# Splitting three weight matrices one layer earlier, and moving a substitution's transfers to the GpSimd queue

## The chip, the cores and the metric

The kernel runs on one core of a Trainium2 chip. The metric is device time in microseconds. The kernel before was timed three times: median 1341.9 us, from 1339.78 to 1342.38 us.

## The reference, cut to what matters

A trunk of four residual sub-layers (token mixer, FFN, token mixer, FFN) on 512 tokens of width 1024, in float32:

```
for i in range(2):
    hn = rms_norm(h, norm_mix_g[i])
    h = h + (sgu_mixer if i == 0 else rwkv7_mixer)(hn, ...)
    h = h + conv_ffn(rms_norm(h, norm_ffn_g[i]), ...)     # (silu(gate) * val) @ w_down, gate, val = conv3(h @ w_up)
return rms_norm(h, norm_final_g)

def rwkv7_mixer(h, ...):             # 16 heads of 64
    xx = token_shift(h) - h
    r, k, v = (h + xx * mu[0]) @ w_r, (h + xx * mu[2]) @ w_k, (h + xx * mu[3]) @ w_v
    w, a, g = low_rank(h + xx * mu[1]), low_rank(h + xx * mu[4]), low_rank(h + xx * mu[5])
    # for each token and head, state S of 64x64:
    #   S = S diag(decay) + (S (-kk)) (kk * a)^T + v k^T ;  y = S r
    y = group_norm(y) * ln_w + ln_b + bonus
    return (y * g) @ w_o
```

The change touches the first FFN (FFN0) and the RWKV-7 mixer behind it.

## The kernel before, in words

**Layout and precision.** Activations stand with 128 features on the partitions and 512 tokens along the row; D = 1024 is 8 such tiles. A float32 product is made of three matmuls on TensorE (`mm3`, lines 240 to 246): both operands are split into a rounded high part and a remainder, and high by high, high by low and low by high are added up. Three matmuls of 128x512 belong to each 128x128 block of a weight.

**Weights.** `weights` (line 221) loads a 512 KB piece from DRAM by the DMA queue of ScalarE (ACT) into `w32` (two buffers), and `split` (line 197) makes the parts of each 512 columns: ACT casts to `wh` (line 205), VectorE (DVE) subtracts to `wl` (line 206), with four buffers each. `Ahead` fetches one weight before it is used.

**FFN0** makes 44 tiles of the up projection, 24 matmuls each, with convolution and gate on DVE and ACT behind them (lines 463 to 470), and then 8 tiles of the down projection.

**RWKV.** `rwkv_first` makes the low-rank terms and r. `rwkv_main` (line 656) is made of generators that `weave` (line 1127) interleaves by `RATES`: a main stream, a side stream and `fill`, which supplies matmuls.

- `projections` is the fill: k and v (16 weights). Each tile of v is followed by `value`: its transposed store (line 738, `vtd`) and a bonus term (line 752). The last four tiles of v belong to head pairs 4 to 7, which the second scan uses.
- `pairs`: for each pair of heads p = 0 to 7 the decay, operands and products of 64-token chunks. They are stored to DRAM scratch by SyncE's queue (SP): `std`, `lpd` (lines 844, 845) and `btd` (lines 856, 858).
- `invert(g)` inverts triangular 64x64 blocks for one group of four pairs: it loads the diagonal 32x32 blocks as `li` (line 898) and the others as `lm` (line 900), substitutes in 31 steps of two DVE operations (lines 910, 911) on a tile `tt`, transposes (lines 918, 919), stores `tt` (line 915), multiplies on TensorE (line 930), copies (line 932) and stores `lm` (line 935). Both groups use the same buffers.
- `scan(g)` runs the recurrence of a group in 8 chunks. Each loads `st`, `vu`, `pt` (from the inverted `lpd`) and `cbt` by SP (lines 954 to 960), and alternates four sets of matmuls (lines 978, 982, 991, 998, 1003) with copies on DVE and ACT. `finish` normalizes two chunks at a time and, twice per group, multiplies by the gate (line 1045 stands in it).
- `project` multiplies by wo, half before all gates are there (group 0), half after (group 1).

The order is: pairs 0 to 3; pairs 4 to 7 with inversion 0 at the side; scan 0 with inversion 1 at the side and the last four tiles of v as fill; scan 1 with `project` as fill; the rest of `project`; FFN1. Tile's scheduler turns that program order into one list of instructions for each engine, and every engine works its list in order.

## Time and profile before

| | |
|---|---|
| three runs, median | 1341.9 us (1339.78 to 1342.38) |
| the profiled execution's own time | 1336.87 us |
| its span in the trace | 1335.0 us |
| TensorE busy | 1269.7 us, 95% of the span |
| DVE, ACT, POOL busy | 842.3, 605.6 and 140.8 us |
| the chain that ended last | 79% TensorE, 8% DVE, 2% ACT, 2% DMA |

TensorE (PE) fills nearly the whole span; the profile page's forty slices show it below 90% in the RWKV stage, from about 600 to 965 us, and at the very ends. A time on the page is a duration in us, or a mean in ns for one instruction. "PE ... x112" counts matmuls; the granted clock (PEclk) is 1.00 at full speed; the DMA share is the mean busy share of the 16 DMA engines and can come out above 1. A name ending in q (SPq, ACTq) is an engine's issuing of a transfer. A bracket behind an instruction tells how long its engine had been idle and what released it.

### The profile page before, as it was taken

The numbers are of one execution on the slowest core, as the hardware profiler recorded it, in microseconds if no ns is written. First come the engines' busy times: TensorE is split into PE (matmuls) and PEld (weight loads), VectorE is DVE, ScalarE is ACT, GpSimd is POOL, SyncE is SP. The second block draws the span as 40 slices with busy tenths as digits, with TensorE's granted clock in tenths as the row PEclk, the third lists the DMA queues.
The fourth block names the chain that finished last, engine by engine and source line by source line (L and its number), as shares of the span: only waits on it lengthen the run. The fifth ranks groups of instructions, "written<-read, shape, count | busy, mean of one in ns | idle before, by whom it ended". The sixth has DMA issues, their size and how long they took to land.

```text
span 1335.0 us, 19041 instructions
## 1 busy us (share of the span) xinstructions
PE 1269.7 (95%) x7490; PEld 1022.9 (77%) x7490; DVE 842.3 (63%) x1349; ACT 605.6 (45%) x1060; POOL 140.8 (11%) x152
## 2 busy tenths in 40 slices
PE   8999999999999999999989848798999999999996
PEld 6778888888888888777766636676888888888886
DVE  5565477777773335957979476556577777772223
ACT  5444354544443333667875424222454545452221
POOL 3100200000000001311210003232300000000001
PEclk9999999999999999999989869899999999999998
DMA  7232333323333333235866796962223333332322
GB/s 260 82 110 79 95 95 95 95 95 97 101 99 103 118 103 99 83 114 128 199 153 171 160 202 151 242 177 79 79 95 95 95 96 99 103 93 87 103 88 75
DMA packets 135786, 156.63 MB, mean 117 GB/s; under 512 B 64976, under 2 KB 100944, under 8 KB 135696
## 3 DMA queue, kind: packets, MB, share of 16 engines
q10 hardware_dynamic: 30688, 101.07, 24.9%
q1 hardware_dynamic: 105008, 54.34, 16.9%
q8 instruction: 59, 0.97, 0.3%
q14 instruction: 31, 0.25, 0.1%
HBM read 130.74 MB, written 24.64 MB: 116 GB/s over the span
## 4 chain that ended last, share of the span: by engine, by line
PE 79%; DVE 8%; ACT 2%; DMA 2%; issue 2%; POOL 1%; SPq 0%; ACTq 0%; DVEq 0%; POOLq 0%
PE mm L244 8%; PE mm L245 8%; PE mm L246 8%; PE e L244 5%; PE e L246 5%; PE e L245 5%; PE us L244 5%; PE us L246 5%; PE us L245 5%; PE aux L244 5%; PE aux L246 5%; PE aux L245 5%; DVE pr L910 1%; DVE tt L911 1%; PE us L978 1%
## 5 line engine op out<-in xcount | busy, mean ns | idle before, releaser
L205 ACT CAST wh<-w 128x512 fp32r<-128x512 f32 (+1 forms) x393 | 239.3, 613 | 441.5 <-PE mm L245 121.0
L206 DVE TENSOR_TENSOR wl<-w,wh 128x512 fp32r<-128x512 f32 (+1 forms) x385 | 267.0, 696 | 206.0 <-ACT wh L205 200.7
L244 PE MATMUL mm<-mxh,wh 128*128 128x512 f32 x424 | 175.1, 413 | 2.7 <-DVE rt L754 2.0
L245 PE MATMUL mm<-mxl,wh 128*128 128x512 f32 x424 | 169.8, 400 | 0.3 <-DVE mxl L1051 0.3
L246 PE MATMUL mm<-mxh,wl 128*128 128x512 f32 x424 | 168.3, 397 | 1.4 <-DVE wl L206 1.4
L271 POOL TENSOR_TENSOR ss<-ss,sq 128x512 f32<-128x512 f32 x30 | 40.4, 1347 | 777.5 <-issue 594.7
L244 PEld LDWEIGHTS mm<-mxh,wh 128*128 128x128 f32 x424 | 80.7, 191 | 25.3 <-issue 4.5
L246 PEld LDWEIGHTS mm<-mxh,wl 128*128 128x128 f32 x424 | 80.5, 190 | 19.2 <-DVE wl L206 2.1
L245 PEld LDWEIGHTS mm<-mxl,wh 128*128 128x128 f32 x424 | 80.7, 190 | 17.7 <-issue 1.4
L465 ACT ACTIVATE cv<-z,par 128x512 f32<-128x512 f32 x88 | 71.7, 817 | 30.4 <-DVE z L463 30.4
L244 PE MATMUL us<-mxh,wh 128*128 128x512 f32 (+1 forms) x216 | 84.5, 391 | 0.1
L244 PE MATMUL e<-mxh,wh 128*128 128x512 f32 x216 | 84.5, 391 | 0.0
L246 PE MATMUL us<-mxh,wl 128*128 128x512 f32 (+1 forms) x216 | 84.1, 389 | 0.0
L245 PE MATMUL us<-mxl,wh 128*128 128x512 f32 (+1 forms) x216 | 84.1, 389 | 0.0
L245 PE MATMUL e<-mxl,wh 128*128 128x512 f32 x216 | 84.0, 389 | 0.0
L246 PE MATMUL e<-mxh,wl 128*128 128x512 f32 x216 | 84.0, 389 | 0.0
L466 DVE SCALAR_TENSOR_TENSOR cv<-z,par,cv 128x512 f32<-128x512 f32 x88 | 66.0, 752 | 24.3 <-ACT cv L465 24.3
L244 PE MATMUL aux<-mxh,wh 128*128 128x512 f32 x208 | 81.2, 391 | 0.1
L246 PE MATMUL aux<-mxh,wl 128*128 128x512 f32 x208 | 81.1, 390 | 0.0
L245 PE MATMUL aux<-mxl,wh 128*128 128x512 f32 x208 | 80.9, 389 | 0.0
L467 DVE SCALAR_TENSOR_TENSOR cv<-z,par,cv 128x512 f32<-128x512 f32 x88 | 66.0, 752 | 2.9
L244 PEld LDWEIGHTS e<-mxh,wh 128*128 128x128 f32 x216 | 40.6, 188 | 8.8 <-issue 0.5
(1062 smaller groups left out, 2499.0 us busy)
## 6 DMA issues: line engine op xcount, KB each, us to landing
w<-in_wup ACTq DMA_DIRECT2D x88, 512.0 KB, 3.6
w<-in_wdn ACTq DMA_DIRECT2D x32, 512.0 KB, 3.6
st<-std SPq DMA_DIRECT2D x16, 512.0 KB, 6.4
w<-in_wdn ACTq DMA_DIRECT2D x16, 384.0 KB, 3.1
w<-in_wsu ACTq DMA_DIRECT2D x8, 512.0 KB, 3.9
w<-in_wso ACTq DMA_DIRECT2D x8, 512.0 KB, 3.6
w<-in_wk ACTq DMA_DIRECT2D x8, 512.0 KB, 4.3
std<-ar SPq DMA_DIRECT2D x16, 256.0 KB, 4.6
```

The source lines that it names most:

```text
L205: nc.scalar.copy(hi[r, :n], src)
L206: (lo_eng or nc.vector).tensor_tensor(lo[r, :n], src, hi[r, :n].bitcast(F32), ALU.subtract)
L244: mm(acc, wh, xh, start=first, stop=False)
L245: mm(acc, wh, xl, start=False, stop=False)
L246: mm(acc, wl, xh, start=False, stop=last)
L271: nc.gpsimd.tensor_tensor(self.ss, self.ss, self.sq, ALU.add)
L465: nc.scalar.activation(c, z[:, 2:], AF.Identity, scale=cw(2, i), bias=self.p("conv_b", l * 44 + i))
L466: nc.vector.scalar_tensor_tensor(c, z[:, 1:T + 1], cw(1, i), c, ALU.mult, ALU.add)
L467: nc.vector.scalar_tensor_tensor(c, z[:, 0:T], cw(0, i), c, ALU.mult, ALU.add)
L910: V.tensor_tensor(q, a, b, ALU.mult)
L911: V.tensor_tensor(tt[:, 0:nj, j + 1:32], tt[:, 0:nj, j + 1:32], q, ALU.add)
L978: nc.tensor.matmul(us[H[hd], 0, i, :], st[:, i, hd, 0:C], vu[:, i, hd, :], start=True, stop=True)
```

## The change

1. **Parts beside FFN0.** `make_parts` is advanced once for each weight of FFN0 (44 times in the up, 4 times in the down projection). A step loads 512 columns of wk, wv or wo by SP, splits them on ACT and DVE and stores both parts to a DRAM scratch `wd`. Its three tiles have one buffer each. In RWKV `parts` loads them: two DMAs on ACT's queue for each 512 columns, into `wh`/`wl`, and every third time into a `w32` buffer. Casts and subtractions of these 24 weights leave the RWKV stage (for wo, half of the subtractions were on POOL), and twice the bytes are loaded there.
2. **Substitution transfers on POOL.** `li` and `lm` are loaded for each pair of heads as it gets ready, by POOL's queue, three DMAs for each pair; the stores of `tt` and `lm` go there too. `lpd` is laid out pair by pair. The two inversions form one side stream.
3. **One store of `bt`** with rows of 512 bytes instead of three stores with rows of 256.
4. **Order.** The loads of scan 0's first chunk, 9 steps of fill and 18 of inversion stand before scan 0; the gates' weights are loaded at the end of the fill; the last `finish` of a scan is carried on in what follows; the reloading of h is written at the head of `project`; the rates change.

```
-RATES = ((1.9, 2), (1.9, 6, 2.2), (0.8, 2, 2), (0.6, 2))
+RATES = ((1.9, 2), (1.9, 6, 2.2), (1, 2, 2), (0.5, 2), (1, 2))
-FIRST0, WAIT, STEPS = 1, 4, (2, 2, 2, 2)
+WAIT, LEAD, STEPS = 2, 9, (2, 2, 2, 2, 2)
+    def make_parts(self, pool):
+        for n in PARTS:                      # ("wk", "wv", "wo")
+            for m in range(KT):
+                for c in (0, 512):
+                    w = pool.tile([P, 512], F32, tag="pw", bufs=1, name=self.uid("pw"))
+                    nc.sync.dma_start(w, self.A[n][m][:, c:c + 512])
+                    for i, x in enumerate(self.split(pool, w, [P, 512], "pw", bufs=1)):
+                        nc.sync.dma_start(self.wd[n][m][:, i, c:c + 512], x.bitcast(F32))
+                    yield
+    def parts(self, blocks):
+        for n, m, c in blocks:
+            self.np += 1
+            if self.np % 3 == 0:
+                w = self.wp.tile([P, 1024], F32, tag="w32", bufs=2, name=self.uid("w32"))
+                x = tuple(w[:, i:i + 512].bitcast(F32R) for i in (0, 512))
+            else:
+                x = tuple(self.wp.tile([P, 512], F32R, tag=tag, bufs=WB, name=self.uid(tag)) for tag in ("wh", "wl"))
+            for i in range(2):
+                self.wq.dma_start(x[i].bitcast(F32), self.wd[n][m][:, i, c:c + 512])
...
-            r.lpd = [dp.tile([NCH, 2, 4, C, P], F32, name=f"lpd{g}") for g in range(2)]
+            r.lpd = [dp.tile([4, NCH, 2, C, P], F32, name=f"lpd{g}") for g in range(2)]
...
         def invert(g):
-            for b in range(2):
-                nc.sync.dma_start(li[H[b]], ld[:, B[b], B[b]])
-            for b in range(2):
-                nc.sync.dma_start(lm[B[b]], ld[B[b], B[0], B[1]].rearrange("u s t -> s u t"))
             G.memset(tt, 0.0)
+            for i in range(4):
+                while 4 * g + i not in done:
+                    yield
+                u = slice(16 * i, 16 * i + 16)
+                for b in range(2):
+                    G.dma_start(li[64 * b + 16 * i:64 * b + 16 * i + 16], ld[u, B[b], B[b]])
+                G.dma_start(lm[B[i // 2], i % 2 * 16:i % 2 * 16 + 16], ld[u, B[0], B[1]].rearrange("u s t -> s u t"))
...
-                nc.sync.dma_start(ld[:, B[b], B[b]], tt[H[b]])
+                G.dma_start(ld[:, B[b], B[b]], tt[H[b]])
...
-                nc.sync.dma_start(ld[B[b], B[0], B[1]].rearrange("u s t -> s u t"), lm[B[b]])
+                G.dma_start(ld[B[b], B[0], B[1]].rearrange("u s t -> s u t"), lm[B[b]])
...
-        inv = invert(0)
+        inv = chain(invert(0), invert(1))
         self.weave(main, inv, fill, *RATES[1], ktiles=STEPS[1])
...
-        inv = invert(1)
-        next(inv)
-        gw = [gate_weights(g) for g in range(2)]
-        s0, s1 = scan(0), scan(1)
-        self.weave(s0, inv, fill, *RATES[2], ktiles=STEPS[2])
+        load(0, 0)
+        for _ in range(LEAD):
+            next(fill, None)
+            next(inv)
+            next(inv)
+        fill = chain(fill, gates())
+        s0 = scan(0)
+        self.weave(s0, inv, fill, *RATES[2], ktiles=STEPS[2], free=True)
...
-        for k in range(KT):
-            nc.sync.dma_start(self.h[k], r.hd[k])
         fill = project()
+        s1 = scan(1, left.pop())
         self.weave(s1, None, fill, *RATES[3], ktiles=STEPS[3])
+        self.weave(left.pop(), None, fill, *RATES[4], ktiles=STEPS[4])
```

On TensorE, where scan 0 begins, the list before read so (mm is a fill product, 978 and 982 the first matmuls of a chunk, 991 the one that needs `pt`):

```order
L246 MATMUL mm_6511<-mxh_5659,wl_6316 128x512
L752 MATMUL mm_6608<-rt_4089,wb_6606 128x512
L978 MATMUL us_6678<-vu_6658,st_6655 64x64
L982 MATMUL e_6679<-vu_6658,st_6655 64x64
L978 MATMUL us_6678<-vu_6658,st_6655 64x64 x7
L982 MATMUL e_6679<-vu_6658,st_6655 64x64 x7
L244 MATMUL mm_6751<-mxh_5447,wh_6514 128x512
L991 MATMUL us_6678<-wt_6688,pt_6656 64x64 x8
```

and the list after, at the same place, so (the lines 978, 982, 991, 998, 1003 are now 1019, 1023, 1032, 1039, 1044; 738 and 752 are 774 and 788):

```order
L279 MATMUL mm_7107<-mxh_6039,wl_7029 128x512
L774 MATMUL mm_7289<-cst,v_7286 128x128 x4
L788 MATMUL mm_7379<-rt_4499,wb_7377 128x512
L1019 MATMUL us_7195<-vu_7003,st_7000 64x64 x8
L1023 MATMUL e_7196<-vu_7003,st_7000 64x64 x8
L1032 MATMUL us_7195<-wt_7205,pt_7001 64x64 x8
L1044 MATMUL e_7196<-vu_7003,pt_7001 64x64
L1039 MATMUL us_7195<-vu_7003,cbt_7002 64x64 x8
L1044 MATMUL e_7196<-vu_7003,pt_7001 64x64 x7
```

Between the last product of the pairs and scan 0 the list now holds 72 fill matmuls, four runs of line 774 and four of line 788, and none of them stand in scan 0's eight chunks any more; the 128 matmuls of inversion 1 (line 968, formerly 930) follow behind its last chunk.

On DVE, where inversion 1 begins, the list before read so (767 and 768 split a weight, 980 is scan 0's first copy, 31 substitution rows later):

```order
L206 TENSOR_TENSOR wl_6755<-w_1285_6752,wh_6754 128x512
L206 TENSOR_TENSOR wl_6759<-w_1285_6752,wh_6758 128x512
L910 TENSOR_TENSOR pr_6626<-li_6623,tt_6625 128x31
L911 TENSOR_TENSOR tt_6625<-tt_6625,pr_6626 128x31
L910 TENSOR_TENSOR pr_6626<-li_6623,tt_6625 128x60
```

and the list after so (1021 and 1033 are scan 0's copies, 948 and 949 the substitution):

```order
L790 TENSOR_TENSOR rt_4499<-mm_7379,v_7286 128x512
L1021 COPY wt_7205<-us_7195 128x256
L948 TENSOR_TENSOR pr_6954<-li_6951,tt_6953 128x31
L1033 COPY vu_7003<-us_7195 64x4x64
L949 TENSOR_TENSOR tt_6953<-tt_6953,pr_6954 128x31
L948 TENSOR_TENSOR pr_6954<-li_6951,tt_6953 128x60
```

Inversion 1 now starts behind scan 0's first copy, with one substitution row ahead of the second, and is spread over seven chunks.

On POOL, where group 0's substitution is stored, the list before held only the clearing of `tt` for group 1 (line 901) after the last bonus product; now it reads:

```order
L858 TENSOR_TENSOR rt_4499<-rt_4499,ss_6522 128x512
L953 DMA lpd_4490<-tt_6209 64x32x32 x2
L931 MEMSET tt_6953 128x1024
L932 MEMSET tt_6953 128x32
L939 DMA li_6951<-lpd_4491 16x32x32
L973 DMA lpd_4490<-lm_6208 32x32x32 x2
L939 DMA li_6951<-lpd_4491 16x32x32
L940 DMA lm_6952<-lpd_4491 32x16x32
L939 DMA li_6951<-lpd_4491 16x32x32 x2
```

The stores of group 0 (lines 953 and 973), the clearing of `tt` and all loads of group 1 stand in one line on POOL, the loads behind the store.

## Rows read from the trace of the kernel before

**Rows 1.** Windows of RWKV: span, busy (instructions) of PE, PEld, DVE, ACT, POOL, clock, DMA share, GB/s
```profile
600.00:757.00 157.00, 149.29 (x1074) 111.60 (x1073) 127.14 (x228) 104.23 (x225) 18.76 (x18) 0.95 0.69 163
757.00:784.00 27.00, 8.42 (x165) 6.61 (x163) 11.75 (x29) 10.64 (x20) 3.17 (x6) 0.72 0.99 199
784.00:855.00 71.00, 59.63 (x985) 46.58 (x983) 46.66 (x105) 24.96 (x58) 16.11 (x19) 0.89 0.79 187
855.00:867.00 12.00, 7.07 (x56) 6.23 (x56) 6.13 (x14) 2.42 (x6) 3.17 (x3) 0.72 1.07 230
867.00:921.00 54.00, 54.00 (x700) 39.46 (x700) 29.64 (x65) 15.22 (x36) 17.42 (x18) 1.00 0.56 150
921.00:965.00 44.00, 39.93 (x184) 32.59 (x183) 27.51 (x41) 19.60 (x36) 15.68 (x15) 0.96 0.23 68
```

**Rows 2.** SP's queue in order of time, end of the pairs: start, us, line, transfer
```profile
754.46 1.93 SPq L915 DMA_DIRECT2D lpd<-tt  x2
...
767.53 3.19 SPq L898 DMA_DIRECT2D li<-lpd  x2
...
774.84 2.82 SPq L954 DMA_DIRECT2D st<-std  x1
```

**Rows 3.** TensorE in order of time, end of the pairs to scan 0
```profile
760.05 1.20 PE L930 MATMUL aux<-li,lm 32*32 32x32 f32 x64
...
764.06 1.02 PE L752 MATMUL mm<-rt,wb 128*128 128x512 f32 x2
783.66 0.37 PE L978 MATMUL us<-vu,st 128*64 128x64 f32 x2 [18.58 <-DMA vu<-vtd]
```

**Rows 4.** FFN0, up projection: a window of 25 us, columns as in rows 1
```profile
250.00:275.00 25.00, 25.00 (x112) 20.69 (x111) 19.33 (x29) 12.85 (x19) 0.00 (x0) 1.00 0.34 104
```

**Rows 5.** FFN0, 175 to 395 us, by line: busy us, mean ns, idle before
```profile
L206 DVE TENSOR_TENSOR wl<-w,wh 128x512 fp32r<-128x512 f32 x82 | 56.2, 686 | 0.7
L205 ACT CAST wh<-w 128x512 fp32r<-128x512 f32 x82 | 51.2, 624 | 79.4 <-PE e L245 23.8 <-PE mm L245 22.3 <-PE us L245 16.6
```

**Rows 6.** DMA issues of the whole span: count, KB each, median us to landing
```profile
hd<-h SPq DMA_DIRECT2D x8, 256.0 KB, 2.1
...
lpd<-tt SPq DMA_DIRECT2D x4, 256.0 KB, 5.4
...
w<-in_g1b ACTq DMA_DIRECT2D x1, 256.0 KB, 2.6
```

**Rows 7.** Pairs and fill, 600 to 757 us, by line
```profile
L206 DVE TENSOR_TENSOR wl<-w,wh 128x512 fp32r<-128x512 f32 x28 | 20.7, 759 | 7.3 <-ACT wh L205 7.3
L205 ACT CAST wh<-w 128x512 fp32r<-128x512 f32 x28 | 16.5, 619 | 12.6 <-PE mm L245 8.8 <-DMA w<-in_wk 1.9 <-DVE pr L910 1.6
```

**Rows 8.** The same stretch, DMA queue of ACT (weights): packets, MB, share of 16 engines
```profile
q10 hardware_dynamic: 2245, 7.43, 16.5%
```

**Rows 9.** Scan 0, TensorE: starts of its last two chunks, which hold no fill
```profile
844.96 0.33 PE L978 MATMUL us<-vu,st 128*64 128x64 f32 x2 [1.22 <-DVE vu L1001]
...
849.59 0.33 PE L978 MATMUL us<-vu,st 128*64 128x64 f32 x2
```

**Rows 10.** The stretch of the last chunk, and one behind it, columns as in rows 1
```profile
850.00:855.00 5.00, 3.43 (x65) 2.69 (x64) 2.56 (x7) 1.12 (x5) 0.53 (x1) 1.00 1.03 370
...
860.00:864.00 4.00, 4.00 (x19) 4.00 (x20) 1.81 (x5) 0.52 (x2) 0.27 (x1) 0.50 1.08 223
```

**Rows 11.** DVE, 776 to 815 us, by line: inversion 1
```profile
L910 DVE TENSOR_TENSOR pr<-li,tt 128x31 f32<-128x31 f32 (+15 forms) x31 | 11.8, 380 | 1.2 <-DMA li<-lpd 0.2
```

**Rows 12.** DMA issues, 757 to 870 us, columns as in rows 6
```profile
pt<-lpd SPq DMA_DIRECT2D x23, 128.0 KB, 5.9
...
lpd<-lm SPq DMA_DIRECT2D x4, 128.0 KB, 3.7
```

**Rows 13.** SP's queue between the scans
```profile
845.71 5.91 SPq L1110 DMA_DIRECT2D h<-hd  x7
```

**Rows 14.** DVE, the end of inversion 0's transposes
```profile
742.51 2.06 DVE L919 STREAM_TRANSPOSE li<-tt 64x1024 f32<-64x1024 f32 x1
```

More of the change, by code (lines that the diff above doesn't have):

```diff
@@ L2 @@
 from contextlib import ExitStack
+from itertools import chain
 import numpy as np
@@ L443, in ffn @@
             nz = 0
+            parts = self.make_parts(fp) if self.next == "rwkv" else iter(())
             def cw(j, i):
@@ L451, in ffn @@
                     w = self.first if i == 0 else self.weights(A["wup"][l, i])
+                    next(parts, None)
                     a = self.acc()
@@ L495, in ffn @@
                     w = self.weights(A["wdn"][l, m][:, k0 * P:(k0 + kn) * P], n=kn * P)
+                    next(parts, None)
                     if m == KT - 1 and k0 == 16:
@@ L690, in projections @@
         def projections():
-            load = Ahead([lambda n=n, m=m: self.weights(A[n][m]) for n in ("wk", "wv") for m in range(KT)])
+            load = Ahead([lambda n=n, m=m: self.parts([(n, m, 0), (n, m, 512)]) for n in ("wk", "wv") for m in range(KT)])
             def key(m, a):
@@ L961, in load, with scan @@
             chunks[g, c] = st, pt, bt, vu
-        def scan(g):
+        left = []
+        def scan(g, late=iter(())):
             ih = [(i, hd) for i in range(4) for hd in range(2)]
-            y, late = None, iter(())
+            y = None
             for c in range(NCH):
                 last = c == NCH - 1
-                if c == 0:
+                if c == 0 and (g, 0) not in chunks:
                     load(g, 0)
@@ L1011, in scan @@
                     late = finish(g, c // 2, y)
-            yield from late
+            left.append(late)
         def finish(g, b, y):
@@ L1058, in load @@
             def load(g, m):
-                return self.weights(A["wo"][m:m + 2, :, 512 * g:512 * g + 512].rearrange("m p c -> p m c"), lo_eng=G)
+                return self.parts([("wo", m + j, 512 * g) for j in range(2)])
             ws = Ahead([lambda g=g, m=m: load(g, m) for g in range(2) for m in range(0, KT, 2)] + [self.prefetch])
+            for k in range(KT):
+                nc.sync.dma_start(self.h[k], r.hd[k])
             for g in range(2):
@@ L1084, in until, with gates @@
                     return
+        gw = []
+        def gates():
+            for g in range(2):
+                with ExitStack() as after:
+                    for eng in (mybir.EngineType.DVE, mybir.EngineType.Activation):
+                        after.enter_context(tc.issue_after(self.last(eng)))
+                    gw.append(gate_weights(g))
+                yield
         fill = projections()
```

37 lines of the change are left out of this document (19 added, 18 removed).

## Prediction

> **What bounds the kernel now.** I read the table of windows by stage first, because TensorE is busy for 95% of the span and only a stage in which it isn't can give time back [rows 1]. In the up projection of FFN0 it runs without a gap at full clock [rows 4], so a gain there is excluded. The reader is to see three holes in RWKV. In the pairs (600 to 757 us) TensorE is busy for 149.29 of 157.00 us at a mean clock of 0.95. Before scan 0 it stands for 18.6 us: its last fill product ends at 765.1 and the first matmul of the scan starts at 783.66 [rows 3]. Scan 0 takes 71.0 us and the way from its end to scan 1 another 12.0, most of it without work [rows 1].
>
> I then read SP's queue over the second hole. The loads of `li` and `lm` for group 1 wait there for the last pair's stores and hold the queue from 767.53 to 774.84; only then is `st` of scan 0 issued, which lands before 783.66 [rows 2, 3]. So the hole belongs to a queue, not to a lack of work: the fill that could have covered it stands behind scan 0's first matmuls on TensorE's list. Scan 0 itself is long because that fill is in it: its last two chunks, which hold none, start 4.63 us apart [rows 9], and eight of these would be 37 us.
>
> **The parts of the change and what they cost.**
>
> *FFN0, 48 part steps.* A window of 25 us holds 112 matmuls [rows 4], so a weight of 24 takes 5.36 us. DVE is busy for 19.33/25 of it, 4.14 us; one more subtraction of 0.69 [rows 5] makes 4.83, 90%. ACT goes from 2.75 to 3.37 us with one more cast of 0.62. Both fit. The step itself has one buffer each, so its parts follow one another: a load of 256 KB, 2.6 us; the cast, 0.62; the subtraction, 0.69; and the issues and signals between, for which I put 0.6. That is 4.5 us, below 5.36, with 0.9 us to spare; the two stores (2.1 us each [rows 6]) run beside the next load. The other end: the four transfers of a step are 1.25 MB where 0.5 MB now makes a DMA share of 0.34, so 0.85 of the period. If they are served one behind the other, the load lands only after 0.85 x 5.36 = 4.6 us of transfers and the 1.7 us by which its 2.6 exceed its own share of them (0.9): 6.2 us. Then TensorE is paced by the step and loses 0.84 us for each of 44 weights, 37 us, less the 8 that three buffered halves (2.7 us each) hide: +29. I take 0, as the rows with durations give 4.5.
>
> *Pairs: no casts and subtractions.* 28 subtractions (20.7 us of DVE) and 28 casts (16.5 us of ACT) go [rows 7]. The stage holds 7.7 us of idle TensorE and, by the clock, about 7.9 more: a gain of 15.6 at most. What remains in the way is the chain from product to mask to store, and the DMA. Fourteen weights with 0.5 MB more each are 7.3 MB; 7.43 MB now take 16.5% of the engines [rows 8], so the share goes from 0.69 to 0.85, and the reloading of h, which the scheduler puts into this stage, adds a little, while the merged `bt` store takes some off. In rows 1 TensorE stands where the share is about 1. I take half of the gain, -7, between -15 and +8 (the idle time doubled).
>
> *From the pairs to scan 0.* Now 72 matmuls of fill (x 0.223 = 16.1 us), four runs of line 788 (1.02 us each [rows 3]) and four of line 774 (taken at the same price, an estimate) stand before the scan: 24.2 us, and about 3.5 us of transposes and inversion 0's last products at 1.20 a run. From 757 that ends at 784.7: where scan 0 began before. The loads for the scan lose the 7.3 us of `li` and `lm` and the 1.93 us of the `tt` store ahead of them on SP [rows 2], so they land some 9 us earlier and the hole is filled with work: 0, the 7 us of the pairs being counted above. Late next would be `li` of group 1, which DVE waits for directly behind the scan's first copy, and `pt`, which waits for the store of group 0's `lm`: both hang on POOL (rival A).
>
> *Scan 0.* Eight bare chunks of 4.63 us are 37. Inversion 1's 62 operations (0.38 us each, 23 us [rows 11]) stand between the scan's copies on DVE, 3.3 us a chunk, of which TensorE's part of a chunk hides some; I take 1.3 us on the path in seven chunks, 9, and the two transposes of 2.06 us whole [rows 14]. That is 50 us. A bare chunk keeps TensorE busy for about 3.4 of 6 us. In the last bare chunk before, 3.43 of 5.00 us were busy and the clock was 1.00; ten us later, after a gap, it was 0.50 [rows 10]. I add 3 us for it: 53 for 71, -18. The ends: no operation on the path, 41 us (-30); and a clock of 0.50 throughout, 2 x 3.43 + 1.2 = 8.1 us a chunk, 69 us (-2).
>
> *From scan 0 to scan 1.* Inversion 1's products now stand behind the last chunk: four runs of 1.20, a copy (about 0.6, as a cast takes [rows 5]), the store by POOL (landing 3.7 for SP's, and 1 for its issue) and 5.9 us from the issue of `pt` to its landing [rows 12]: 16 us, beside which the gates run. It was 12.0, with the reloading of h in SP's queue, 5.91 us [rows 13], now gone ahead. I take +4, between 0 and +8.
>
> *Scan 1 and the rest of the projection.* Scan 1 had TensorE busy for 54.00 of 54.00 us, and 39.93 of 44.00 follow [rows 1]. 24 matmuls (5.4 us) move from the first stretch into the second, and the gates of group 0 into the first; the last gates have 26 fill matmuls before them for 14. Zero, give or take 4. Halving the stores of `bt` and the shorter subtraction list of wo are off the path.
>
> The price of a transfer that POOL issues has no row. The nearest: SP's issue of half a `tt`, 2048 pieces of 128 bytes, took 0.96 us (0.5 ns a piece) [rows 2], and its landing 5.4 us (2.6 ns a piece, if POOL were to spend all of that time on them) [rows 6]. I take 1 ns, nearer to the issue, as landing includes the memory's answer; at either end the sum above moves by 2 us at most (rival A shows how).
>
> The Trainium skill ("DMA: Bandwidth & Descriptors", section "SWDGE vs HWDGE vs iDMA") says that a transfer issued from GpSimd gets its descriptors from a program on its cores and one from SP or ACT from hardware, and (section "Anatomy of one DMA") fits 2.0 us + bytes/436 GB/s to the former: 2.6 us for half a `tt`, where the rows have 5.4 for SP's; by that fit the stores would come out faster and the sum 2 or 3 us lower, but it has no term for pieces of 128 bytes, and no run here shows one.
>
> **The sum.** 0 - 7 + 0 - 18 + 4 + 0 = -21 us on an execution of 1336.9 us (span 1335.0), which is 5.0 below the median of the runs: 1315.9 there, 1321 as a median. Its own range is 1303 to 1334.
>
> **The rivals.**
>
> *A. POOL's queue is late (slower).* Inversion 0 ended on DVE at 744.6 [rows 14], say 737.6 now. Behind it POOL has in one line: 4096 pieces of `tt`, their landing (5.4 us) before `tt` is cleared, 2048 pieces of `lm`, and 6144 pieces of group 1's loads; DVE goes on in scan 0 when the last has landed (another 5.4). That is 748.4 us + 12288 pieces: at 2.4 ns a piece it meets the first copy of the scan at about 778. Above, each ns costs 12.3 us there, and about 6 more at the second handover, where 6144 pieces of stores stand before `pt`. The gain of 21 is used up at 3.3 ns a piece; at 4 ns scan 0 starts 20 us later and scan 1 another 9: +8, 1350. For it: the pieces are small and the transfers in a line. Against: POOL is busy for 18.76 of 157 us in the pairs [rows 1], and half of the loads belong to pairs that are long done. The Trainium skill ("SBUF — State Buffer", section "SBUF: two separate sides") adds a cause of the same lateness: certain DVE operations on float32 lock GpSimd out while it writes descriptors; no row here shows such a transfer, so nothing bears it out.
>
> *B. The part step paces FFN0 (slower or little gained).* The cycle of 4.5 us has 0.9 us to spare. For it: three transfers more per weight, on a share of 0.34, and DVE at 90%, whose list has the subtraction in a fixed place, so that a late load holds the convolution too. Against: 2.6 and 2.1 us are measured with other transfers about. At 6.0 us a step the loss is 0.64 x 44 - 8 = 20 us and the whole comes out at 1341; at 6.2, 1350; at 5.7, 1328.
>
> *C. The wait changes its place.* Scan 0 stays near 69 us at a low clock and the pairs, with DMA at 0.85, give nothing: -2 + 0 + 4, so 1342 to 1344. For it: where TensorE is half idle the clock is 0.72 [rows 1]. Against: the bare chunks had 1.00.
>
> **Chances and range.** The forecast 0.53, A 0.17, B 0.20, C 0.10. 0.2% is 2.7 us and about what a measurement of this kernel can tell from no change. Faster: all of the forecast but 0.02, 0.01 of A, 0.09 of B, 0.02 of C: 0.63. Within 0.2%: 0.01 of the forecast, 0.02 of B and 0.04 of C: 0.07. Slower: the rest, 0.30. The range reaches to 1303 below and to 1356 above, which takes in B's end and A up to 4.3 ns a piece.
>
> **What would show it.** In FFN0 TensorE without a gap and part steps a period of 5.4 us apart; gaps there, ended by DVE or by a `pw` load, would be B. In the pairs a window some 7 us shorter, DMA share about 0.85. TensorE without a long stand before scan 0; chunks of about 6 us with clock 0.8 or more (C if 8 or more); the first row of inversion 1 without a wait for `li`, and scan 1's first `pt` product about 16 us behind scan 0's end. A wait of ten us or more for `li` or `pt`, or POOL's issues of several us each, would be A and make the prediction wrong.

## The result, and the profile after

The change made the kernel slower: 1346.87 us in the median of five runs (1345.87 to 1347.52) beside 1340.13 for the kernel before on the same chip, a ratio of 1.0047 with a 95% interval of 1.0032 to 1.0061. The forecast was 1321 us. The profiled execution took 1345.87 us, its span 1344.1, where before had 1336.87 and 1335.0.

Six marks on the engines' time lines, found in both traces, cut the span: the last addition to h in FFN0, the starts of the first and the last product of the pairs, scan 0's first matmul, scan 1's first product with `pt`, and the last group of scan 1's products.

| stretch | before, us | after, us | difference | forecast |
|---|---|---|---|---|
| start to the end of FFN0 | 519.4 | 525.3 | +5.9 | 0 |
| to the first products of the pairs | 97.6 | 101.3 | +3.7 | none |
| pairs, first to last products | 131.6 | 131.5 | -0.1 | -7 |
| to scan 0's first matmul | 35.1 | 46.5 | +11.4 | 0 |
| scan 0 to scan 1's first `pt` product | 83.5 | 74.2 | -9.3 | -18 + 4 |
| scan 1 | 52.9 | 51.4 | -1.5 | 0 |
| the rest of the span | 414.9 | 413.9 | -1.0 | 0 |

Two thirds of the gain of 14 us forecast from scan 0 to scan 1 came; the pairs gave nothing, and three other stretches lost more than was gained. The windows of the changed kernel by these stretches (from the end of FFN0 on), columns as in [rows 1]:

```profile
525.25:626.55 101.30, 99.30 (x446) 77.84 (x445) 67.09 (x90) 57.98 (x104) 21.36 (x21) 0.98 0.38 110
626.55:758.00 131.45, 123.93 (x897) 93.64 (x898) 101.80 (x185) 80.96 (x177) 27.12 (x30) 0.92 0.87 226
758.00:804.50 46.50, 34.45 (x326) 25.70 (x322) 3.46 (x5) 14.45 (x31) 12.04 (x20) 0.82 0.97 232
804.54:878.73 74.19, 50.41 (x941) 43.38 (x941) 50.53 (x127) 20.24 (x46) 19.60 (x23) 0.72 0.69 186
878.73:930.85 52.12, 50.91 (x699) 39.20 (x699) 31.44 (x73) 12.81 (x33) 14.89 (x16) 0.93 0.50 137
```

The stand of 18.6 us before scan 0 [rows 3] is filled with work in part, as foreseen, yet the stretch is longer: TensorE still stands for 12 of 46.5 us. The DMA share of the pairs, 0.87, is what the forecast had (0.85). But the pairs are no shorter, at a mean clock of 0.92.

**FFN0.** The window of [rows 4] in the changed kernel, and one at the end of the up projection:

```profile
250.00:275.00 25.00, 25.00 (x112) 20.71 (x111) 21.55 (x33) 14.13 (x24) 0.00 (x0) 1.00 0.75 238
...
400.00:425.00 25.00, 23.07 (x96) 17.29 (x95) 13.64 (x22) 10.13 (x18) 0.00 (x0) 1.00 0.70 204
```

The steps' transfers between 175 and 395 us (columns as in [rows 6]), and who waited for the loads (us in total, times, longest):

```profile
w<-in_wup ACTq DMA_DIRECT2D x38, 512.0 KB, 4.2
pw<-in_wv SPq DMA_DIRECT2D x16, 256.0 KB, 3.5
...
wkd<-pwl SPq DMA_DIRECT2D x13, 256.0 KB, 3.3
pw<-in_wk SPq DMA_DIRECT2D x12, 256.0 KB, 3.8
```
```profile
ACT pwh L211 <- DMA pw<-in_wv: 20.9, 14, 3.2
ACT pwh L211 <- DMA pw<-in_wk: 20.1, 11, 2.8
```

The first and the 44th load of the steps, on SP:

```profile
153.60 0.33 SPq L247 DMA_DIRECT2D pw<-in_wk  x1
...
398.38 0.45 SPq L247 DMA_DIRECT2D pw<-in_wo  x1
```

The load lands after 3.5 to 3.8 us, not 2.6, and ACT stands before the cast `pwh` for it. By the forecast's own sum the step is then 3.6 + 0.62 + 0.69 + 0.6 = 5.5 us; the loads of the first 44 are in fact 5.69 us apart on average, over the period of 5.36. The loss shows late: up to 275 us the windows are as dense as before, three of 25 us between 275 and 400 us hold 108 matmuls for 112, and the one at 400 us, the start of the down projection, holds 96 where the kernel before has 109. TensorE waits there for casts of FFN0's own weights. ACT, which takes its list in order, stands before a `pwh` meanwhile:

```profile
ACT pwh L211 <- DMA pw<-in_wo: 14.2, 5, 5.5
...
PE e L277 <- ACT wh L211: 1.8, 2, 1.0
```

**Pairs.** Windows of 6 us with the two holes of the stage, and the waits for a DMA in the whole stage:

```profile
662.50:668.50 6.00, 3.64 (x29) 2.58 (x30) 1.41 (x3) 1.21 (x3) 2.22 (x3) 0.91 1.10 287
668.50:674.50 6.00, 5.44 (x29) 4.33 (x28) 3.37 (x6) 5.59 (x14) 1.54 (x3) 0.52 0.94 235
...
686.50:692.50 6.00, 3.08 (x24) 2.34 (x24) 5.63 (x8) 5.15 (x15) 1.79 (x3) 0.90 0.78 184
692.50:698.50 6.00, 6.00 (x44) 5.64 (x44) 2.23 (x5) 3.52 (x8) 2.36 (x4) 0.50 1.06 280
698.50:704.50 6.00, 5.48 (x22) 3.60 (x19) 3.98 (x11) 1.10 (x2) 0.00 (x0) 0.50 0.95 222
```
```profile
DVE lq L879 <- DMA std<-lq: 12.7, 6, 4.3
ACT vt L779 <- DMA wh<-wvd: 2.9, 1, 2.9
PEld mm L279 <- DMA w<-wkd: 2.5, 1, 2.5
```

In each hole TensorE is idle for two to three of 6 us, and behind each the granted clock is 0.50 to 0.52, the lower of its two levels, for 6 to 12 us: these holes are paid for twice. In the first one DVE waits 4.34 us to overwrite `lq`, whose store by SP has not landed, and a weight comes 2.36 us late. DVE's waits for these stores are 12.7 us in the stage.

**From the pairs to scan 0.** SP's queue, then ACT, then TensorE in order of time, as in [rows 2] and [rows 3]:

```profile
776.88 0.72 SPq L992 DMA_DIRECT2D st<-std  x1
783.88 1.28 SPq L995 DMA_DIRECT2D pt<-lpd  x2
788.53 0.38 SPq L780 DMA_DIRECT2D vtd<-vt  x1
```
```profile
793.93 0.36 ACT L779 COPY vt<-mm 64x256 f32<-64x256 f32 x1 [9.57 <-DMA vtd<-vt]
```
```profile
795.53 2.05 PE L788 MATMUL mm<-rt,wb 128*128 128x512 f32 x2 [8.33 <-issue]
...
804.54 0.69 PE L1019 MATMUL us<-vu,st 128*64 128x64 f32 x16
```

Read backwards: TensorE stands 8.33 us ahead of a bonus product, and the profile names no releaser; ACT's last copy out of the tile before it ended at 795.42, so I take it that TensorE waited for that. ACT stands 9.57 us before it may overwrite `vt`, whose store is behind `pt` on SP; and SP issued nothing for 6.3 us before `pt`. What SP waited for there:

```profile
SPq L995 <- DMA wh<-wod: 6.7, 2, 6.1
```

This is the landing of a part of wo that ACT had loaded: issued at 775.58, landed at 783.79. POOL's stores of `lpd` were not it: POOL saw them landed at 772.48.

**Scan 0 and POOL.** The answer to [rows 11], the first two and the last issue of `li` on POOL, and landings (the first of these answers to [rows 12]):

```profile
L948 DVE TENSOR_TENSOR pr<-li,tt 128x31 f32<-128x31 f32 (+15 forms) x31 | 11.5, 371 | 0.7
```
```profile
765.36 0.63 POOL L939 DMA_DIRECT2D li<-lpd  x1 [1.74 <-PE aux L968]
...
768.21 0.63 POOL L939 DMA_DIRECT2D li<-lpd  x1
...
778.43 0.63 POOL L939 DMA_DIRECT2D li<-lpd  x1 [0.27 <-DMA lm<-lpd]
```
```profile
pt<-lpd SPq DMA_DIRECT2D x22, 128.0 KB, 4.1
...
li<-lpd POOLq DMA_DIRECT2D x8, 64.0 KB, 6.9
lpd<-lm POOLq DMA_DIRECT2D x4, 128.0 KB, 4.0
```

A load of 512 pieces takes POOL 0.63 us, and the last `li`, issued at 778.43, landed at 788.5, 17 us before DVE's first use of it at 805.7, which waited for nothing. Rival A, a late POOL, is excluded.

From scan 0 on, TensorE, DVE and ACT in order of time:

```profile
820.25 0.69 DVE L212 TENSOR_TENSOR gw_1412l<-w,gw_1412h 128x512 fp32r<-128x512 f32 x1 [6.23 <-ACT gw_1412h L211]
...
826.50 0.69 DVE L212 TENSOR_TENSOR gw_1425l<-w,gw_1425h 128x512 fp32r<-128x512 f32 x1 [2.29 <-ACT gw_1425h L211]
```
```profile
819.60 0.62 ACT L211 CAST gw_1412h<-w 128x512 fp32r<-128x512 f32 x1 [5.60 <-DMA w<-in_g]
```
```profile
821.62 0.48 PE L1019 MATMUL us<-vu,st 128*64 128x64 f32 x2 [5.51 <-DVE vu L1042]
...
858.49 6.81 PE L968 MATMUL aux<-li,lm 32*32 32x32 f32 x256 [0.82 <-DVE li L956]
...
878.73 0.30 PE L1032 MATMUL us<-wt,pt 64*64 64x64 f32 x2 [2.24 <-DMA pt<-lpd]
```

DVE stands 6.23 and 2.29 us, and the scan's copies on its list with it, before it may split the gates' weights (`gw`): ACT waits for their loads, which it issued only at 812.47 and later. Two chunks of the scan take 12.4 and 11.2 us there. The change had put these loads at the end of the fill (part 4), and they fell between scan 0's copies. Inversion 1's products (line 968) ran ahead of the eighth chunk, whose matmuls stand behind 866 us, and not behind it as the section on the change has it. The first seven chunks took 53.1 us.

### The profile page after: what moved, and what is told of

Its sections match the earlier page's. It is cut to its first block, busy times and chain, and to the rows that moved or that the text cites. A ratio compares the mean times of both kernels' runs of the same rounds, so it can differ in the third digit from the quotient of the medians.

```text
span 1344.1 us, 19490 instructions
## 1 busy us (share of the span) xinstructions
PE 1277.0 (95%) x7490; PEld 1030.4 (77%) x7490; DVE 837.6 (62%) x1357; ACT 601.7 (45%) x1068; POOL 153.0 (11%) x176
## 4 chain that ended last, share of the span: by engine, by line
PE 60%; DMA 14%; DVE 11%; issue 5%; ACT 4%; SPq 1%; POOL 1%; ACTq 0%; DVEq 0%; POOLq 0%
PE mm L277 7%; PE mm L278 6%; PE mm L279 6%; PE us L277 4%; PE us L278 4%; PE e L279 4%; PE e L277 4%; PE e L278 4%; PE us L279 4%; PE aux L277 3%; PE aux L278 3%; PE aux L279 3%; DMA pw<-in_wo 3%; DMA pw<-in_wk 3%; DMA pw<-in_wv 2%
## 5 line engine op out<-in xcount | busy, mean ns | idle before, releaser
L212 DVE TENSOR_TENSOR wl<-w,wh 128x512 fp32r<-128x512 f32 x345 | 235.3, 684 | 186.2 <-ACT wh L211 181.8
L211 ACT CAST wh<-w 128x512 fp32r<-128x512 f32 x345 | 207.3, 609 | 315.5 <-PE us L278 78.6
L277 PE MATMUL mm<-mxh,wh 128*128 128x512 f32 x360 | 147.1, 409 | 0.0
L278 PE MATMUL mm<-mxl,wh 128*128 128x512 f32 x360 | 143.3, 398 | 0.0
L279 PE MATMUL mm<-mxh,wl 128*128 128x512 f32 x360 | 142.9, 397 | 0.3 <-DVE wl L212 0.3
L277 PEld LDWEIGHTS mm<-mxh,wh 128*128 128x128 f32 x360 | 68.8, 191 | 17.8 <-issue 3.7
L279 PEld LDWEIGHTS mm<-mxh,wl 128*128 128x128 f32 x360 | 68.6, 190 | 16.5 <-DVE wl L212 1.4
L278 PEld LDWEIGHTS mm<-mxl,wh 128*128 128x128 f32 x360 | 68.8, 191 | 14.4 <-issue 1.2
L211 ACT CAST pwh<-pw 128x512 fp32r<-128x512 f32 x48 | 29.8, 621 | 76.4 <-DMA pw<-in_wo 29.5
```

The costliest lines, as they stand in the source:

```text
L211: nc.scalar.copy(hi[r, :n], src)
L212: (lo_eng or nc.vector).tensor_tensor(lo[r, :n], src, hi[r, :n].bitcast(F32), ALU.subtract)
L277: mm(acc, wh, xh, start=first, stop=False)
L278: mm(acc, wh, xl, start=False, stop=False)
L279: mm(acc, wl, xh, start=False, stop=last)
```

## The experiments

All were timed against the kernel before on the same chip. "To scan 0" is from the last product of the pairs to scan 0's first matmul. The stages are those of one profile each, so a verdict rests on the ratio.

| kernel | median, us | ratio to before, 95% | pairs, us | to scan 0, us |
|---|---|---|---|---|
| after | 1346.9 | 1.0047 (1.0032 to 1.0061) | 131.5 | 46.5 |
| no_parts | 1341.0 | 1.0018 (1.0003 to 1.0032) | 133.3 | 40.1 |
| parts_only | 1343.8 | 1.0049 (1.0030 to 1.0068) | 129.9 | 37.8 |
| parts_pool | 1333.9 | 0.9963 (0.9945 to 0.9982) | 115.9 | 45.1 |
| parts_only_pool | 1336.6 | 0.9996 (0.9979 to 1.0013) | 117.1 | 36.7 |
| one_dma | 1348.9 | 1.0088 (1.0068 to 1.0107) | 137.1 | 44.2 |
| act_sliver | 1348.0 | 1.0082 (1.0055 to 1.0108) | 131.1 | 48.9 |
| act_touch | 1331.5 | 0.9948 (0.9927 to 0.9968) | 114.5 | 44.2 |
| act_touch512 | 1340.0 | 1.0003 (0.9982 to 1.0023) | 124.7 | 44.8 |
| dummy_act | 1333.1 | 0.9966 (0.9946 to 0.9986) | 117.9 | 45.7 |
| vtd_pool | 1341.0 | 1.0017 (1.0000 to 1.0034) | 131.3 | 44.3 |
| pp_vtd_act | 1324.9 | 0.9900 (0.9865 to 0.9935) | 112.4 | 41.1 |
| no_parts_vtd | 1336.8 | 0.9991 (0.9975 to 1.0007) | 133.7 | 44.1 |
| part_ahead | 1344.5 | 1.0043 (1.0021 to 1.0065) | 131.9 | 47.3 |
| lo_pool | 1365.9 | 1.0206 (1.0180 to 1.0233) | 128.9 | 50.0 |
| best2 | 1328.8 | 0.9946 (0.9927 to 0.9965) | 120.0 | 39.4 |
| parts_only_mix | 1332.7 | 0.9956 (0.9933 to 0.9980) | 119.6 | 37.2 |
| mix_vtd_act | 1326.2 | 0.9917 (0.9893 to 0.9940) | 117.6 | 35.9 |
| best3 | 1324.6 | 0.9895 (0.9864 to 0.9926) | 119.4 | 45.9 |

**The two halves.** no_parts is the change without the parts; parts_only is the kernel before with the parts alone.

```
# no_parts: no step beside FFN0; k, v and wo are loaded and split as before
-            parts = self.make_parts(fp) if self.next == "rwkv" else iter(())
+            parts = iter(())
-    Ahead([lambda n=n, m=m: self.parts([(n, m, 0), (n, m, 512)]) ...
+    Ahead([lambda n=n, m=m: self.weights(A[n][m]) ...
```

> The changed kernel with its weights loaded and split in RWKV as before; no part steps in FFN0. What is left of the change is the substitution on POOL, the one bt store and the new order. Against the changed kernel (1346.9 us) the trace puts 5.9 us of loss in FFN0, 3.7 ahead of the first products, 1.6 in the pairs and 9.8 between the last products and scan 0, and a gain of 14.4 from scan 0 to scan 1. Theory 1 (the parts cost it all: their steps pace FFN0, and their four transfers per weight hold ACT's and SP's queues before scan 0): 1326 to 1331, scan 0 starting within 30 us of the last products. Rival (the new order itself costs the handover, because fill is put before a scan that could have covered it): only FFN0 comes back, 1339 to 1342, and the 46 us from the last products to scan 0 stay.

> The kernel before with the first part of the change alone: part steps in FFN0, parts loaded by ACT in RWKV; substitution, bt store and order as before. Theory 1 (four transfers a weight on ACT's queue hold ACT and SP; FFN0 loses 3 to 6 us): the pairs gain nothing, 1342 to 1347 where the kernel before has 1339. Rival (the casts were what held the pairs, and only the new order spoilt it): 1327 to 1333.

Most of the loss is the parts' (+0.49%); the new order alone is worth nothing, or a loss of 0.2%: what the way from scan 0 to scan 1 gains (77.8 us for 83.5), the stretch before it loses (40.1 for 35.1).

**Who issues the loads of the parts.** Same bytes, same buffers; POOL in place of ACT, once in the changed kernel and once in the old order.

```
-                self.wq.dma_start(x[i].bitcast(F32), self.wd[n][m][:, i, c:c + 512])          # after, parts_only
+                self.nc.gpsimd.dma_start(x[i].bitcast(F32), self.wd[n][m][:, i, c:c + 512])   # parts_pool, parts_only_pool
```

> The changed kernel with the loads of the parts issued by POOL in place of ACT; same bytes, same buffers. Theory 1a (the loads hold ACT, because a transfer waits for an earlier one of either hardware queue to land before it is issued, and ACT's copies and SP's loads stand behind): the 8.3 us wait for vt before line 788 and the 2.5 us wait for line 970 go, 1334 to 1340. Rival 1b (it is the doubled bytes on full DMA engines, which any queue would feel): 1345 to 1350, the waits only change their place.

> The same as parts_only with the parts loaded by POOL. With parts_pool the pairs took 115.9 us for 129.9 before. Theory 1 (the gain of the parts is there once their loads leave ACT's queue, and the new order gives nothing beside it): 1328 to 1333, no slower than parts_pool's 1334. Rival 2 (the new order is worth its 14 us from scan 0 to scan 1 and the parts pay only with it): 1337 to 1343.

That is 0.84% in the new order and 0.53% in the old one. In both the pairs are shorter, by 15.6 and 12.8 us; in the old order the way from scan 0 to scan 1 gave half of it back (93.4 us for 85.8). The windows of parts_pool, the first two by the stages, then the longest hole of its pairs and what follows:

```profile
623.90:739.90 116.00, 108.64 (x875) 82.64 (x874) 93.55 (x173) 76.22 (x169) 47.07 (x66) 0.99 0.91 238
739.90:785.00 45.10, 30.45 (x328) 22.66 (x324) 3.46 (x5) 13.75 (x29) 15.72 (x27) 0.89 0.92 205
...
645.00:648.50 3.50, 0.50 (x14) 0.36 (x12) 1.74 (x5) 3.47 (x11) 0.27 (x1) 1.00 1.04 273
648.50:654.50 6.00, 6.00 (x49) 4.32 (x45) 4.92 (x7) 1.49 (x3) 4.61 (x7) 1.00 0.84 194
```

The DMA engines are busier than in the changed kernel (0.91 for 0.87), and the pairs are 15.7 us shorter than before, just past the upper end of the gain that the forecast gave them. So doubled bytes are not what kept the gain away. TensorE is idle for as long in these pairs as in the changed kernel's, 7.4 and 7.5 us. The difference is its busy time, 108.6 us for 123.9, at a mean clock of 0.99 for 0.92, and with some 22 matmuls fewer, as part of the fill stands ahead of the first products here (in the old order the clock was 1.00 for 0.95). A hole of 3 us was followed by full clock here. The Trainium skill ("DMA: Bandwidth & Descriptors", section "Issuing engines are not separate DMA queues") says that starting transfers from several engines only saves the sequencer's time for starting them, usually small beside the transfer. The runs differ: to move the issue to another engine was worth 13 us. It is not the issue alone that moved: in the profile POOL's transfers also go through another queue, q0 for SP's and ACT's q10.

What about ACT's issuing is it? Between the first products and scan 0 the changed kernel's ACT issued 53 transfers, 23.3 us, and stood idle for 18.3 us just before them (kernel before: 18 transfers, 6.4 and 3.5 us); the expectations below have 52, 27.8 and 22.9, which the trace does not give. one_dma halves the number, one load of both parts.

```
+                w = self.wp.tile([P, 2, 512], F32R, tag="whl", bufs=WB, name=self.uid("whl"))
+            self.wq.dma_start(w.bitcast(F32), self.wd[n][m][:, :, c:c + 512])
```

> The changed kernel with both parts of 512 columns in one tile, loaded by one transfer on ACT's queue in place of two: same bytes, half as many transfers for ACT to issue. Theory 1a (it is the number of transfers that hold ACT and SP, each waiting for an earlier one to land): about half of what POOL's queue gave in the pairs, 131.5 to 122 to 126 us, and 1336 to 1342. Rival 1c (ACT is held by the waits of its loads for free buffers, however many they are): the pairs stay at 129 to 133 us, 1344 to 1349.

ACT's share fell to 14.8 and 4.4 us, and nothing was gained: the number alone is not the cause. Next, a dummy load of 64 bytes by ACT beside each of POOL's.

```
+                d = self.gp.tile([1, 16], F32, tag="dum", bufs=6, name=self.uid("dum"))
+                self.wq.dma_start(d, self.A[n][m][0:1, 0:16])
```

> parts_pool (0.9963 of the kernel before) with a transfer of 64 bytes, which nothing reads, issued by ACT behind each of POOL's loads of parts: ACT has as many issues as in the changed kernel, and SP's and ACT's transfers take turns with them, but nothing that ACT issues is large or waits for a weight's buffer. In the changed kernel ACT spent 27.8 us on 52 issues and 22.9 us idle right before them between the first products and scan 0, where the kernel before spent 6.4 and 3.5. Theory 1a (issuing and taking turns is what holds ACT): 1342 to 1348, the pairs back at 128 us or more. Rival 1c (it is the wait for buffers that TensorE frees): 1333 to 1337, the pairs within 4 us of parts_pool's 115.9.

This run says nothing on the question: the scheduler put the dummy loads, which depend on nothing, between 23 and 208 us, none of them in RWKV. In act_sliver ACT loads 16 rows of each part and POOL the other 112, so that both wait for the same buffer.

```
+                for eng, r in ((self.wq, slice(0, 16)), (self.nc.gpsimd, slice(16, P))):
+                    eng.dma_start(x[i][r].bitcast(F32), self.wd[n][m][r, i, c:c + 512])
```

> The kernel with all loads of the parts on POOL came out at 1333.9 us, with all on ACT at 1346.9, at the same bytes. Here each load is divided: ACT issues rows 0 to 15 (an eighth of the bytes), POOL rows 16 to 127. Theory: what costs is that ACT, an in-order engine with the pairs' copies on its list, stops at a load until its buffer is free; it stops just so for an eighth of the rows. Then the pairs (first to last products) take 128 us or more, ACT stands for some 20 us before its loads between the first products and scan 0, and the time is 1342 to 1348 us. Rival: it is how the rows are shared among the queues and engines, or ACT's issue time by bytes: then it stays near the kernel with POOL alone, 1333 to 1338 us, with pairs near 117 us.

An eighth of the bytes costs as much as all of them (25.0 us of issue, 12.6 idle). So it isn't bytes. My theory, that ACT's stops for free buffers are the cost, was met in the time but not yet separated from the issue; act_touch does that. ACT writes a constant into each tile just before POOL loads it, act_touch512 into all of it.

```
+                self.nc.scalar.copy(x[i][:, 0:P], self.c("ident", P))     # act_touch
+                self.nc.scalar.copy(x[i], self.cst[:, 0:512])             # act_touch512
                 self.nc.gpsimd.dma_start(x[i].bitcast(F32), self.wd[n][m][:, i, c:c + 512])
```

> All loads of the parts stay on POOL (1333.9 us, with 161 us from the first products to scan 0), but ahead of each load ACT copies 128x128 constants into the tile that will be loaded; the load overwrites them. So ACT stops at the same 52 places until the same buffers are free, and the loads follow it, but ACT issues no transfer of a part and its issue time (27.8 us in the changed kernel) is replaced by short copies. Theory: the stop of an in-order ACT is what costs 13 us: 1342 to 1348 us, 175 us or more from the first products to scan 0. Rival: it is the issuing (ACT's issue time, or transfers of SP and ACT waiting for one another to land): 1333 to 1338 us, 160 to 165 us.

> As the kernel with 128x128 copies by ACT ahead of each of POOL's part loads (1331.5 us), but with copies of the whole 128x512 tile, about 0.6 us each: 52 of them are some 32 us of ACT between the first products and scan 0, more than the 27.8 us that ACT spent there on issuing the parts in the changed kernel, with the stops for buffers besides. Theory: the cost of ACT's loads is not ACT's time but that transfers of SP and ACT wait for one another's landing in turn: still within 1329 to 1338 us. Rival: it is ACT's time, and the short copies were too short to show it: 1342 us or more.

The copies of act_touch between 620 and 790 us (count, ns shortest, median, longest), and what POOL's loads waited for:

```profile
L263 ACT CAST wl<-cst x20: 283/297/312, 622.4 to 782.9; 128x128 fp32r<-128x128 f32 x20
L263 ACT CAST wh<-cst x19: 282/297/314, 625.6 to 782.0; 128x128 fp32r<-128x128 f32 x19
L263 ACT CAST w<-cst x14: 284/298/302, 626.0 to 729.8; 128x128 fp32r<-128x128 f32 x14
...
  POOL wh L264: 35.9, 10
  POOL wl L264: 6.1, 1
```

ACT stopped for the same buffers at the same places, and the loads followed it, yet the time stayed that of parts_pool. My theory of the stops fell. The long copies (0.62 us each, 34 us in all with 4 idle) cost 0.55% against the short ones, intervals apart: ACT's time counts once there is more of it. But they reached neither the changed kernel nor act_sliver (1.0082), where ACT gave 38 us to transfers. So more than ACT's time is in it, and that goes with transfers on SP's and ACT's queues. In the built program these share eight completion signals in turn: each waits for an earlier one of either engine to land. The trace agrees for the wait of 6.1 us above: SP's `pt` was issued 0.09 us after the landing of ACT's load of wo, and both report to the same signal. A stretch of ACT's list and one of SP's in the changed kernel:

```
L263 DMA wh_5320<-wkd_66 128x512 [waits DMAHW2_49]
L263 DMA wl_5321<-wkd_66 128x512 [waits DMAHW4_49]
...
L880 DMA lpd_4491<-lq_6186 64x4x128 [waits DMAHW2_49,DVE_49]
L881 DMA std<-lq_6186 64x4x128 [waits DMAHW3_49]
```

POOL's transfers have signals of their own. Of ACT's 18.3 us of standing before its loads in the changed kernel, 15.0 ended with such a landing and only 3.2 with TensorE's freeing of a buffer, so the stops for buffers of my theory were short from the start. From the first products to scan 0 SP waited 31.0 us, 25 times, for a DMA in the changed kernel, 19.7 us, 14 times, in act_sliver, and 4.1 us, twice, in parts_pool. DVE's wait for `std<-lq` (12.7 us above) was 6.9 in parts_pool, 1.7 in act_touch and 9.8 in act_touch512. This fits a coupling of the two queues; it isn't shown as the cause: no run gave them separate signals, in one_dma SP's waits were short (14.7 us, 7 times) while the time was not, and in parts_only they were long (50.6 us) while DVE's wait was 1.8. No run tried POOL's queue with ACT's signals, or SP as the issuer, so what of POOL's issuing gives the 13 us stays open.

**The store of v.** In the changed kernel it stands behind `pt` on SP. vtd_pool issues it from POOL; pp_vtd_act from ACT, in parts_pool; no_parts_vtd from ACT, in no_parts.

```
-            nc.sync.dma_start(vtd[:, :, m].rearrange("c p f -> p c f"), vt)
+            nc.scalar.dma_start(vtd[:, :, m].rearrange("c p f -> p c f"), vt)   # vtd_pool: nc.gpsimd
```

> The changed kernel with the store of vt to vtd issued by POOL in place of SP. In the trace SP's queue stood behind the first pt load from 777.6 to 783.9 and issued the vt store at 788.5, ACT could not overwrite vt until it landed (9.6 us), and TensorE waited 8.3 us at line 788. Theory (SP's order is what makes that wait): 1337 to 1341. Rival (the store lands late on any queue, as the DMA is full, or the wait just moves to the scan's loads): 1345 to 1349.

> parts_pool with the store of vt issued by ACT, which makes vt. In parts_pool that store was issued by SP among the scan's loads at 760.3, landed at about 775, ACT stood 12.9 us and TensorE 11.5 us at line 788. Theory (SP's list delays it): that wait falls below 3 us, 1323 to 1327. Rival (the DMA engines are full then, and the store lands late from any queue): 1331 to 1336.

> no_parts (new order and POOL's substitution, weights as before; 1.0018 of the kernel before) with the store of vt issued by ACT. In no_parts TensorE stood 4.8 us at line 788 for it. Theory (the new order moves fill out of scan 0 into the hole ahead of it, so TensorE's idle time in RWKV is about the same, and only this wait stands against a small gain): 1331 to 1336, 0.994 to 0.998 of before. Rival (the order is a loss by itself, as scan 0 runs at a clock of 0.66 and scan 1 takes 8 us more): 1337 or more.

On ACT with the parts on POOL it gains 0.6%, the intervals apart; on POOL (0.3%) and without the parts the intervals overlap. SP's and ACT's side of the longest wait in parts_pool:

```profile
760.30 0.57 SPq L780 DMA_DIRECT2D vtd<-vt  x1
...
762.08 9.02 SPq L995 DMA_DIRECT2D pt<-lpd  x1
```
```profile
775.51 1.50 ACT L779 COPY vt<-mm 64x256 f32<-64x256 f32 x4 [12.93 <-DMA vtd<-vt]
```

The longest of these in pp_vtd_act is 6.18 us. Here the store was issued ahead of the long issue of `pt`, and landed only 15.1 us later. In pp_vtd_act the stores still took 8.9 and 12.1 us to land, but ACT issues them right behind its copies. So `pt` on SP holds the store in the changed kernel but not in parts_pool; in both, the late landing holds ACT and through it TensorE's fill. Why the store lands late was not found.

**FFN0's step.** part_ahead loads the next 512 columns ahead of the stores, in two buffers; lo_pool gives the subtraction to POOL; best2 is pp_vtd_act with part_ahead and the first block in `w32`.

```
+                ahead = load(*todo[k + 1])                                                  # part_ahead
+            for i, x in enumerate(self.split(pool, w, [P, 512], "pw", bufs=1, lo_eng=nc.gpsimd)):  # lo_pool
+            if self.np % 3 == 1:                                                            # best2
```

> The changed kernel with two buffers for the loaded columns of a part step, and the next load issued before the stores of the present one. Theory (one load of 3.6 us, cast, subtraction and issues one behind the other make a step of 5.5 us, which paces FFN0): FFN0 ends 5 to 6 us earlier, 1341 to 1342. Rival (DVE at 83% and ACT's list, or the DMA engines at 0.73, are what slows FFN0): no more than 1.5 us, 1345 to 1348.

> The changed kernel with the subtraction of the part steps on POOL, which has nothing to do in FFN0, in place of DVE. FFN0 ended 5.9 us later than before (in three variants 3.2 to 3.7 us), and two buffers for the load did not help. Theory 3 (DVE's list, busy 80 to 84%, makes convolution and split late for TensorE): FFN0 ends 2 to 5 us earlier, 1341 to 1344. Rival (the full DMA delays FFN0's own weights, or ACT's list does): no change, 1345 to 1348.

> pp_vtd_act (0.990 of the kernel before) with the part steps' loads one ahead, and with the first 512 columns of wk loaded into a w32 buffer, which is free before wh and wl are. In the changed kernel the first product of k began 3.7 us after the last product of the low-rank stage, for the load had to wait for wh and wl. Theory: FFN0's end to the first products of the pairs takes 98 us for 101, FFN0 ends within 3 us of before, 0.985 to 0.989, 1317 to 1323. Rival (the third columns wait in its place): 0.988 to 0.992.

In part_ahead the steps' loads are 5.09 us apart, and FFN0 had no loss from 250 to 400 us; but it lost 3 us early, no net gain. In lo_pool, where the subtraction takes 1.30 us for 0.69, they are 6.01 us apart, and FFN0 ended at 539.55 us, 20 us later than before and 14 later than after: a longer step paces FFN0. best2 did not shorten the start of RWKV (102.3 us) and is behind pp_vtd_act.

**The best of both orders.** With wo's loads back on ACT: parts_only_mix and mix_vtd_act in the old order, best3 in the new.

```
+                (self.wq if n == "wo" else self.nc.gpsimd).dma_start(x[i].bitcast(F32), ...)
```

> parts_only_pool (0.9996) with wo's parts loaded by ACT again, as POOL also makes the scans' first products of state and decay and stood behind wo's loads; order and substitution as in the kernel before. Its first products to scan 0 took 153.8 us (166.6 before), its scans 145.0 (136.4 before). Theory (the new order is worth nothing, the pairs' gain is all): scans back at 136 to 138, 1325 to 1330. Rival (the new order carries part of pp_vtd_act's gain): 1331 to 1336.

> The old order of the substitutions (as before the change) with the parts beside FFN0, the loads of k's and v's parts on POOL, wo's on ACT, and the transposed stores of v on ACT. Theory: the new order of the substitutions and its transfers on POOL brings the 14 us that it takes out of the stretch from scan 0 to scan 1 back into the stretch before it, so it is worth little: this kernel then stands within 4 us of the one with the new order and the same queues (1324.6 us): 1321 to 1329. Rival: the order carries a gain of its own once the store of v is no longer late: then this kernel stays at 1331 to 1337, as without the moved store (1332.7).

> pp_vtd_act (0.990) with wo's parts loaded by ACT. In parts_pool a load of wo on POOL stood ahead of POOL's product for scan 0's second chunk and TensorE waited 5.5 us there. Theory: 2 to 5 us less, 0.986 to 0.989, 1319 to 1323. Rival (ACT is held by them in scan 1 instead): 0.989 to 0.993.

best3, with pp_vtd_act level, beats both kernels: 1324.6 us, 1.1% below before. mix_vtd_act, with the old order, lies 0.2% behind it, within the intervals. So the order brings nothing measurable even with the queues at their best; the gain is the parts', issued by POOL, and the store of v on ACT.

## Why the prediction was wrong

- **Pairs, -7.** Failed. The casts and subtractions went and the DMA share rose as expected, but the step counted the parts' transfers as bytes alone, not as 53 issues on ACT. parts_pool has the gain and more (-16, just past the end of -15), so the missing term was who issues. It priced 53 issues of ACT and what they wait for at nothing; with them TensorE stood no longer than with POOL's, but was busy longer at a clock of 0.92 for 0.99. Why ACT's issuing does this is open.
- **From the pairs to scan 0, 0.** Failed. +11.4. The hole of [rows 3] was filled in part, and the step named `pt` as late next, but put it down to POOL and asked only who needs `pt`. It did not ask what is queued behind `pt` on SP: the store of v, ACT's copy and the fill that was to cover the hole. Waits of 8.33 us on TensorE and 9.57 us on ACT came of it. In the changed kernel `pt` itself waited 6.1 us for a load of ACT's. Inversion 0's last products, put at 3.5 us, took 6.9.
- **FFN0, 0.** A term of the wrong size. The load was taken from a row of a quiet stretch (2.6 us [rows 6]) and took 3.6 at the share of 0.75 that the change makes. That is rival B with a step of 5.69 us: by B's own sum 0.33 x 44 - 8 = 6.5 us, measured +5.9; for lo_pool's 6.01 the sum gives 20.6, measured 20.2. Steps and weights keep pace with each other, so the spacing alone gives no direction; lo_pool, where the step was made longer, does. The other kernels with the parts ended FFN0 from 0.1 us earlier to 5.5 later than before, so a step so near the period may cost nothing.
- **Scan 0 and the way to scan 1, -18 + 4.** In part: -9.3, at a clock of 0.72, not 0.8 or more. Seven chunks took the 53.1 us that the step had for eight (53), and from there to scan 1's `pt` it was 21.0 us for 16, with the eighth chunk in it. No term stood for the gates' weights, whose loads came between scan 0's copies: DVE stood 6.23 and 2.29 us for them, and two chunks took 12.4 and 11.2 us where the step had some 6. Inversion 1's products stood ahead of the eighth chunk and not behind it. TensorE was busy for only 50.4 of 74.2 us, and the clock had been 0.86 in the same stretch before; that the missing fill lowered it is argued, not shown.
- **The start of RWKV.** +3.7 was not in the sum. It comes with the parts: this stretch took 97.6 us in the kernels without them, 100.6 to 103.8 in all with them. The last low-rank products stood 1.92 us at 602.36 and the k products behind them ran at about half speed at first; why wasn't settled by a run.
- **Rivals.** A was excluded. B came at its small end. C came in part: the pairs gave nothing and scan 0 ran at a low clock, but its chunks lost a part of their gain to the gates' weights, and the largest loss stood ahead of scan 0.

## What to carry to other kernels

When a change trades arithmetic for transfers, count the issuing instructions on the engine that issues them and try another queue before giving up the trade; here that was 13 us at equal bytes, though it was not found which part of the other queue did it. When a wait is moved, list what stands behind it in the same queue, not only who needs it. Fill moved into a hole leaves a hole where it was; here the clock there was 0.72 for 0.86. When loads are moved to "the end of the fill", look whose list their waits then stand on.

## What the runs showed of the hardware that was not expected

- Two holes of two to three us in TensorE's work were followed by 6 to 12 us at half clock (the windows at 662 and 686 us); one of 3 us in parts_pool was followed by full clock (645 us).
- POOL issued a load of 512 pieces of 128 bytes in 0.63 us; its bulk load of 128x512 took 0.54 us, ACT's 0.33.
- One issue on SP took 9.02 us (`pt` in parts_pool), where most of the same line took about 0.6; the cause wasn't looked for.
